# The inverse transform of a depthwise convolution written with tokens on partitions, its LayerNorm there, and transposes back

## The chip, the cores and the metric

The kernel runs on one core of a Trainium2 chip. The metric is the device time of one execution in microseconds (us), as the median of the runs. Engines are named as in the profile: PE is TensorE (PEld its weight loads), DVE VectorE, ACT ScalarE, POOL GpSimd, SP the engine whose queue issues most of the DMAs.

## What is computed

Two layers over 512 tokens of width 1024 (8 grid rows of 64 tokens). Layer 0 is a gated recurrence, and the change leaves it alone. Layer 1 is a convolution module; from the reference, cut:

```python
def _conv_mixer(h, w_in, b_in, dw, dw_b, ln_g, ln_b, w_out, b_out, conv_fn):
    p = h @ w_in + b_in
    a, gl, gate = jnp.split(p, 3, axis=-1)          # 2048 channels each
    u = a * jax.nn.sigmoid(gl)
    u = conv_fn(u, dw, dw_b)                        # 31 taps along each grid row of 64 tokens, plus dw_b
    u = jax.nn.silu(_layernorm(u, ln_g, ln_b))      # mean and variance over the 2048 channels
    return (u * jax.nn.silu(gate)) @ w_out + b_out
...
    x = x + gate[:, None] * y
...
return _rmsnorm(x, final_norm_g)
```

## The kernel before

All data is float32. A product that must be exact to float32 is made of three products of two parts each (`hi`, `lo`, type float32r); a few small products are plain float32 matmuls, which the profile shows as two passes, so two rows for one matmul.

Layer 1 (from line 656) works in four groups `g` of 512 channels:

- **Two halves of the input projection** (lines 679 to 701): `part` 1 is the gate `gl`, `part` 0 the value `a`. Each has 96 products of 128x512 into four PSUM banks `pa{part}_{g}_{t}`, one for each 128 tokens `t`. The pool `pa` has four banks, so the first product of the next half needs the first bank to have been read. Weights come in four pieces `ci{part}_{g}_{kq}`: a DMA on SP into `raw`, a copy to `hi` on ACT (line 139), a subtraction to `lo` on POOL or DVE (line 141). `raw`, `hi` and `lo` have three buffers each.
- **The reading of the banks** (lines 702 to 716, DVE and ACT) adds the biases of the group, which lie in the tile `bb`: `bb[:, 1]` for `gl` (line 704, into `sgl`), `bb[:, 0]` for `a` (line 710, into `ta`). `bb` has one buffer; a DMA that POOL issues (line 675) fills it with the group's 512 channels, the same for all partitions. Then `u` is made, one tile for each grid row, with the high part of the row on one half of the partitions and the low part on the other.
- **The transform** (lines 718 to 723): for each grid row `r` a bank `pf` gets two products, one with `f_hi` over all 128 partitions, one with `f_lo` over the 64 partitions of the high part. DVE multiplies it with the transformed taps `wt`, which gives `pr` (118 x 512).
- **The inverse** (lines 724 to 734): for each 128 channels `ct` a bank `pi` gets eight products, 128 columns of `pr` as weights and the 64 columns of `inv` moving. The channels are then on partitions. ACT adds the bias, DVE sums `s1` for the mean.

Two pieces of a modulation vector (`ada_piece`, lines 170 to 180: a DMA into `raw`, a chain of eight DVE instructions `adacc`, a product `adbps`) follow in each group.

After the groups comes the **LayerNorm** (lines 741 to 763): the mean is a product with `ones` over `s1`, then 16 subtractions (DVE), 16 squares (ACT), 14 additions on DVE and POOL, two products `var`, a logarithm and an exponential, 16 multiplications (DVE) and 16 SiLUs (ACT). The **gate path** (lines 767 to 781) has 24 products `pgt` for each of 16 tiles `ct`; its weights `cg` are split with `lo` on POOL. `z = gate * y` goes, in two parts, into the output projection `cop` (line 824 on).

A scheduler sets the order of instructions on each engine. It puts the transform and inverse of group `g` between the input products of group `g + 1`, and those of group 3 between the first gate products.

## Time and profile before

| | |
|---|---|
| median of 3 runs | 1392.67 us (1392.63 to 1394.99) |
| span of the profiled execution | 1389.6 us |
| PE busy | 1332.2 us, 96% of the span |
| DVE, ACT, POOL busy | 962.8, 637.4, 368.9 us |
| mean granted clock of PE | 0.986 of full |
| DMA | 119 MB, mean 86 GB/s |

The page gives the span of the profiled execution, from its first to its last instruction, and no time of its own beside it; the median of the three runs is 3.07 us above that span. A busy PE is one with at least one matmul in its pipeline: the distance from one matmul's start to the next one's start tells what a matmul costs, the duration in a row is longer.

### The profile page before, as it was taken

Reading aid. Unit: us, or ns where it says so; the run is one execution under the profiler, and the core shown is the slowest. Engines: PE = TensorE matmul, PEld = TensorE weight load, DVE = VectorE, ACT = ScalarE, POOL = GpSimd, SP = SyncE. Lnnn points to the kernel's source line nnn. Section 1 sums busy time; section 2 is a strip of 40 time slices with the busy share of each in tenths; the row PEclk is TensorE's granted clock in tenths of the full one; section 3 lists DMA queues with packets and bytes.
Section 4 is the critical chain, followed back from the end, with each engine's and each line's share of the span. In section 5 each row is a group of like instructions: output and inputs, shape, how many; then the busy total and the mean of one; then the engine's idle time right before and its main releaser. Section 6 shows DMA issues by size and latency. Waiting matters only on the chain.

```text
span 1389.6 us, 18990 instructions
## 1 busy us (share of the span) xinstructions
PE 1332.2 (96%) x7530; PEld 1124.9 (81%) x7530; DVE 962.8 (69%) x1486; ACT 637.4 (46%) x965; POOL 368.9 (27%) x302
## 2 busy tenths in 40 slices
PE   6999999999999999999999999999999999986997
PEld 2588988998888898888898889867787877865887
DVE  8868787896687786787688777756656747278323
ACT  6455553562355354465345455443223333458321
POOL 3222241240240151140033133122211213267221
PEclk9999999999999999999999999999999999998999
DMA  9312113114112312212211312023422322120321
...
DMA packets 35720, 119.05 MB, mean 86 GB/s; under 512 B 4562, under 2 KB 6898, under 8 KB 35632
## 3 DMA queue, kind: packets, MB, share of 16 engines
...
## 4 chain that ended last, share of the span: by engine, by line
PE 61%; DVE 22%; ACT 5%; DMA 4%; POOL 4%; issue 3%; SPq 0%; DVEq 0%; ACTq 0%; POOLq 0%
PE pa L688 4%; PE pa L689 4%; PE pa L693 4%; PE pz L301 2%; PE pz L302 2%; PE pz L304 2%; PE pi L728 2%; PE cop L842 2%; PE cop L846 2%; PE cop L843 2%; PE op L530 2%; PE h_sc L465 2%; DVE adacc L176 2%; PE op L532 2%; PE op L531 2%
## 5 line engine op out<-in xcount | busy, mean ns | idle before, releaser
L688 PE MATMUL pa<-ci_hi,h_hi 128*128 128x512 f32 x256 | 99.6, 398 | 1.9 <-ACT h_hi L649 1.9
L689 PE MATMUL pa<-ci_lo,h_hi 128*128 128x512 f32 x256 | 100.4, 396 | 0.0
L116 POOL TENSOR_SCALAR sg<-sg 128x1536 f32<-128x1536 f32 x16 | 76.6, 4787 | 70.7 <-ACT sg L549 70.5
L301 PE MATMUL pz<-h_hi,wz_hi 128*128 128x512 f32 x232 | 93.3, 402 | 0.8 <-ACT wz_hi L139 0.8
L302 PE MATMUL pz<-h_lo,wz_hi 128*128 128x512 f32 x232 | 92.9, 401 | 0.0
L176 DVE SCALAR_TENSOR_TENSOR adacc<-adb,sc,adacc 128x128 f32<-128x128 f32 x224 | 82.0, 384 | 3.6
L141 POOL TENSOR_TENSOR ci_lo<-ci_raw,ci_hi 128x1024 fp32r<-128x1024 f32 x18 | 44.5, 2472 | 144.4 <-ACT ci_hi L139 124.6
L141 POOL TENSOR_TENSOR cg_lo<-cg_raw,cg_hi 128x1024 fp32r<-128x1024 f32 x16 | 62.2, 3889 | 66.9 <-PE pgt L774 28.2
L139 ACT ACTIVATE ci_hi<-ci_raw 128x1024 fp32r<-128x1024 f32 x29 | 30.7, 1059 | 93.8 <-PE pa L693 53.6
L693 PE MATMUL pa<-ci_hi,h_lo 128*128 128x512 f32 x224 | 72.1, 400 | 0.0
L312 PE MATMUL pv<-wv_hi,h_hi 128*128 128x256 f32 x256 | 64.8, 288 | 0.0
L313 PE MATMUL pv<-wv_hi,h_lo 128*128 128x256 f32 x256 | 64.1, 286 | 0.0
L400 POOL TENSOR_TENSOR h_f<-h_fac 128x16 f32<-128x16 f32 x16 | 10.0, 627 | 198.6 <-DVE h_kl L446 147.1
L304 PE MATMUL pz<-h_hi,wz_lo 128*128 128x512 f32 x232 | 61.3, 399 | 0.0
L432 DVE SCALAR_TENSOR_TENSOR h_S<-h_S,h_dec,h_kb 128x128 f32<-128x128 f32 x96 | 48.7, 507 | 18.0 <-ACT h_kb L426 16.9
L139 ACT ACTIVATE wz_hi<-wz_raw 128x1024 fp32r<-128x1024 f32 x29 | 30.7, 1057 | 64.6 <-DMA wz_raw<-in_w_in 51.7
L302 PE MATMUL pc<-hc,wz_hi 128*128 128x256 f32 x232 | 60.1, 291 | 0.0
L301 PE MATMUL pc<-hc,wz_hi 128*128 128x256 f32 x232 | 59.7, 289 | 0.0
L688 PEld LDWEIGHTS pa<-ci_hi,h_hi 128*128 128x128 f32 x256 | 48.2, 188 | 13.5 <-issue 2.7
L141 DVE TENSOR_TENSOR wz_lo<-wz_raw,wz_hi 128x1024 fp32r<-128x1024 f32 x29 | 35.4, 1222 | 32.3 <-ACT wz_hi L139 32.1
L689 PEld LDWEIGHTS pa<-ci_lo,h_hi 128*128 128x128 f32 x256 | 48.2, 188 | 11.3 <-issue 0.7
L377 POOL TENSOR_TENSOR h_ref<-h_tot,h_gt 128x64 f32<-128x64 f32 x16 | 17.5, 1091 | 146.4 <-DVE h_ref L404 136.7
...
## 6 DMA issues: line engine op xcount, KB each, us to landing
adb<-in_ada_c SPq DMA_DIRECT2D x32, 512.0 KB, 3.4
ci_raw<-in_c_in SPq DMA_DIRECT2D x32, 512.0 KB, 3.4
wz_raw<-in_w_in SPq DMA_DIRECT2D x29, 512.0 KB, 3.4
ada<-in_ada_a SPq DMA_DIRECT2D x16, 512.0 KB, 7.2
wv_raw<-in_w_v SPq DMA_DIRECT2D x16, 512.0 KB, 3.4
wg_raw<-in_w_in SPq DMA_DIRECT2D x16, 512.0 KB, 3.4
cg_raw<-in_c_gate SPq DMA_DIRECT2D x16, 512.0 KB, 3.5
co_raw<-in_c_out SPq DMA_DIRECT2D x16, 512.0 KB, 3.5
```

The costliest lines, as they stand in the source:

```text
L116: (G if pool_min else V).tensor_scalar(out=t, in0=t, scalar1=EMAX, scalar2=None, op0=ALU.min)
L139: act(out=hi, in_=raw, func=AF.Copy)
L141: lo_eng.tensor_tensor(out=lo, in0=raw, in1=hi.bitcast(F32), op=ALU.subtract)
L176: V.scalar_tensor_tensor(out=acc, in0=raw[:, k, :], scalar=sc[:, k, 0:1], in1=acc, op0=ALU.mult, op1=ALU.add)
L301: mm(ps[:, :T], lhsT=hi[:, k, :], rhs=rhi[k], start=(k == 0), stop=False)
L302: mm(ps[:, :T], lhsT=hi[:, k, :], rhs=rlo[k], start=False, stop=False)
L304: mm(ps[:, :T], lhsT=lo[:, k, :], rhs=rhi[k], start=False, stop=(k == KD - 1))
L312: mm(ps[:, :256], lhsT=lhi[k][:, c], rhs=hi[:, k % 4, :], start=(k == 0), stop=False)
L313: mm(ps[:, :256], lhsT=llo[k][:, c], rhs=hi[:, k % 4, :], start=False, stop=False)
L688: mm(pss[t], lhsT=h_hi[:, 2 * kq + k, c], rhs=hi[:, k, :], start=(kq == 0 and k == 0), stop=False)
L689: mm(pss[t], lhsT=h_hi[:, 2 * kq + k, c], rhs=lo[:, k, :], start=False, stop=False)
L693: mm(pss[t], lhsT=h_lo[:, 2 * kq + k, c], rhs=hi[:, k, :], start=False, stop=(kq == 3 and k == 1))
```

## The change

Of layer 1 alone, and of the host's layout of one small array:

- `f_lo` becomes a tile of two matrices with zeros in the half that isn't wanted, so that both products of the transform run over all 128 partitions.
- The inverse has `inv` as weights and `pr` as moving operand. Two grid rows go to the two column halves of the array and so to the two partition halves of one bank `py`; tokens are then on partitions. Two matmuls of 64x512 for a bank of 128 tokens stand for eight of 128x64 for a bank of 128 channels.
- The bias of the convolution is added by DVE from a third row of `bb`, `bb[:, 2]`; `bb` grows from 512 to 768 KB and still has one buffer.
- Mean and variance come from `bn_stats` and `bn_aggr`; 16 `tensor_scalar` normalise. The products `mean` and `var`, the squares and the sums are gone.
- Each `ct` has four TensorE transposes into a bank `pt`, which ACT reads with the SiLU.
- Every second `lo` of the gate weights moves from POOL to DVE; `gate` has 4 buffers where it had 8 and 8; the pool of `y` has 20 where it had 16.

```diff
-        f_lo = p1.tile([P, P], F32R, name="f_lo")
+        f_lo = p1.tile([P, 2, P], F32R, name="f_lo")
+        V.memset(f_lo.bitcast(F32), 0.0)
         V.tensor_copy(out=f_hi, in_=fraw)
-        V.tensor_tensor(out=f_lo, in0=fraw, in1=f_hi.bitcast(F32), op=ALU.subtract)
+        for i in range(2):
+            o = slice(i * GRID, (i + 1) * GRID)
+            V.tensor_tensor(out=f_lo[o, i, :], in0=fraw[o], in1=f_hi[o].bitcast(F32), op=ALU.subtract)
+        eye1 = p1.tile([P, P], F32, name="eye1")
+        nc.sync.dma_start(out=eye1, in_=consts[:, C_IDN:C_IDN + P])
...
-                bb = pu.tile([P, 2, 512], F32, name=f"bb{g}", tag="bb", bufs=1)
+                bb = pu.tile([P, 3, 512], F32, name=f"bb{g}", tag="bb", bufs=1)
                 nc.gpsimd.dma_start(out=bb, in_=c_bab[:, :, g * 512:(g + 1) * 512].partition_broadcast(P))
...
-                for r in range(ROWS):
-                    ps = pf.tile([P, 512], F32, name=f"pf{g}_{r}", tag="pf")
-                    o = slice((r % 2) * GRID, (r % 2 + 1) * GRID)
-                    mm(ps, lhsT=f_hi, rhs=u[r], start=True, stop=False)
-                    mm(ps, lhsT=f_lo[o, :], rhs=u[r][o, :], start=False, stop=True)
-                    V.tensor_tensor(out=pr[r][:NR], in0=ps[:NR], in1=wt[g][:NR], op=ALU.mult)
-                for i in range(4):
-                    ct = 4 * g + i
-                    ps = pm.tile([P, 512], F32, name=f"pi{ct}", tag="ms")
-                    for r in range(ROWS):
-                        mm(ps[:, r * GRID:(r + 1) * GRID], lhsT=pr[r][:NR, i * P:(i + 1) * P], rhs=inv[:NR, :], start=True, stop=True)
-                    y.append(p1.tile([P, L], F32, name=f"y{ct}", tag="y", bufs=NH))
-                    act(out=y[ct], in_=ps, func=AF.Identity, bias=ccols[:, 0, ct:ct + 1])
-                    ...
+                for t in range(NB):
+                    py = pm.tile([P, 512], F32, name=f"py{g}_{t}", tag="ms")
+                    for i in range(2):
+                        r = 2 * t + i
+                        ps = pf.tile([P, 512], F32, name=f"pf{g}_{r}", tag="pf")
+                        mm(ps, lhsT=f_hi, rhs=u[r], start=True, stop=False)
+                        mm(ps, lhsT=f_lo[:, i, :], rhs=u[r], start=False, stop=True)
+                        pr = pu.tile([P, 512], F32, name=f"pr{g}_{r}", tag="pr", bufs=8)
+                        V.tensor_tensor(out=pr[:NR], in0=ps[:NR], in1=wt[g][:NR], op=ALU.mult)
+                        mm(py[i * GRID:(i + 1) * GRID], lhsT=inv[:NR, :], rhs=pr[:NR], start=True, stop=True)
+                    yt[t, g] = p1.tile([P, 512], F32, name=f"yt{g}_{t}", tag="y", bufs=20)
+                    V.tensor_tensor(out=yt[t, g], in0=py, in1=bb[:, 2, :], op=ALU.add)
+                    V.bn_stats(out=stats[t][:, g, :], in_=yt[t, g])
...
-        (mean, 16 subtractions, 16 squares, 14 additions, var, 16 multiplications, 16 SiLUs)
+        for t in range(NB):
+            V.bn_aggr(out=mv[:, t, :], in_=stats[t].rearrange("p a b -> p (a b)"))
+        act(out=rst, in_=mv[:, :, 1:2], func=AF.Ln, bias=eps)
+        act(out=rst, in_=rst, func=AF.Exp, scale=-0.5)
+        for g in range(4):
+            for t in range(NB):
+                V.tensor_scalar(out=yt[t, g], in0=yt[t, g], scalar1=mv[:, t, 0:1], scalar2=rst[:, t, :], op0=ALU.subtract, op1=ALU.mult)
...
-            w = wpiece(c_gate[ct], [KD, P], f"cg{ct}", G)
+            w = wpiece(c_gate[ct], [KD, P], f"cg{ct}", (V, G)[ct % 2])
...
+            ps = pm.tile([P, 512], F32, name=f"pt{ct}", tag="ms")
+            for t in range(NB):
+                nc.tensor.transpose(ps[:, t * P:(t + 1) * P], yt[t, ct // 4][:, (ct % 4) * P:(ct % 4 + 1) * P], eye1)
+            y = pg.tile([P, L], F32, name=f"y{ct}", tag="yc", bufs=4)
+            act(out=y, in_=ps, func=AF.Silu, scale=ccols[:, 2, ct:ct + 1], bias=ccols[:, 3, ct:ct + 1])
```

How the scheduler's order moves, at three places. Line numbers after the change are 6 higher up to the biases' additions (704 and 710 become 710 and 716), and L733 is the product `py`, L735 the addition into `yt`.

PE, where `part` 1 of group 1 (banks `pa_1_0` to `pa_1_3`) ends and `part` 0 begins with its first bank; before:

```order
L689 MATMUL pa_1_3_9014<-ci_1_3_lo,h_hi 128x512
L693 MATMUL pa_1_3_9014<-ci_1_3_hi,h_lo 128x512 x2
L688 MATMUL pa_1_0_9143<-ci_1_0_hi,h_hi 128x512
L689 MATMUL pa_1_0_9143<-ci_1_0_lo,h_hi 128x512
L728 MATMUL pi_8921<-tr,pr_6_8887 128x64
L728 MATMUL pi_8933<-tr,pr_6_8887 128x64
```

and after the change:

```order
L699 MATMUL pa_1_3_8997<-ci_1_3_hi,h_lo 128x512 x2
L733 MATMUL py_3_8936<-pr_6_8940,tr 64x512
L178 MATMUL adbps_8963<-ones,adacc_8954 128x1
L733 MATMUL py_3_8936<-pr_7_8946,tr 64x512
L178 MATMUL adbps_8977<-ones,adacc_8968 128x1
L694 MATMUL pa_1_0_9126<-ci_1_0_hi,h_hi 128x512
L695 MATMUL pa_1_0_9126<-ci_1_0_lo,h_hi 128x512
```

The last inverse product of group 0 now stands between the two parts, and `part` 0 starts right behind it. Groups 1 and 2 read alike.

The queues of POOL and DVE at the same place (names with all numbers; the first digit of `ci` is the part, the last the piece). POOL before:

```order
L141 TENSOR_TENSOR ci1_1_2_lo_9079<-ci1_1_2_raw_9075,ci1_1_2_hi_9077 128x1024
L675 DMA bb1_8997<-in_c_bab 128x2x512
L141 TENSOR_TENSOR ci0_1_0_lo_9151<-ci0_1_0_raw_9147,ci0_1_0_hi_9149 128x1024
L141 TENSOR_TENSOR ci0_1_2_lo_9211<-ci0_1_2_raw_9207,ci0_1_2_hi_9209 128x1024
L141 TENSOR_TENSOR ci1_2_0_lo_9433<-ci1_2_0_raw_9429,ci1_2_0_hi_9431 128x1024
```

POOL after:

```order
L141 TENSOR_TENSOR ci1_1_2_lo_9062<-ci1_1_2_raw_9058,ci1_1_2_hi_9060 128x1024
L141 TENSOR_TENSOR ci0_1_0_lo_9134<-ci0_1_0_raw_9130,ci0_1_0_hi_9132 128x1024
L141 TENSOR_TENSOR ci0_1_2_lo_9194<-ci0_1_2_raw_9190,ci0_1_2_hi_9192 128x1024
L681 DMA bb1_8980<-in_c_bab 128x3x512
L141 TENSOR_TENSOR ci1_2_0_lo_9392<-ci1_2_0_raw_9388,ci1_2_0_hi_9390 128x1024
```

The load of `bb` for group 1 has moved behind the weight pieces of `part` 0. DVE after, from the last addition that reads `bb0` to the first that reads `bb1` (`adacc27` is the chain of a modulation piece whose DMA also lands here):

```order
L735 TENSOR_TENSOR yt0_3_8949<-py0_3_8936,bb0_8590 128x512
L176 SCALAR_TENSOR_TENSOR adacc26_9344<-adb26_9342,sc_100,adacc26_9344 128x128
L180 TENSOR_TENSOR adac_113<-adbps25_8977,ab_88 128x1
L736 BN_STATS st3_8586<-yt0_3_8949 128x6
L176 SCALAR_TENSOR_TENSOR adacc26_9344<-adb26_9342,sc_100,adacc26_9344 128x128 x6
L174 TENSOR_SCALAR adacc27_9358<-adb27_9356,sc_100 128x128
L176 SCALAR_TENSOR_TENSOR adacc27_9358<-adb27_9356,sc_100,adacc27_9358 128x128 x5
L710 TENSOR_TENSOR sgl1_0_8982<-pa1_1_0_8994,bb1_8980 128x512
L710 TENSOR_TENSOR sgl1_1_8983<-pa1_1_1_8995,bb1_8980 128x512
```

Before, the last reader of `bb0` was the addition of line 710 for the fourth 128 tokens of group 0, some 14 instructions ahead of the first reader of `bb1` on DVE.

PE among the input products of group 1, after the change, where an inverse product stands alone:

```order
L695 MATMUL pa_1_3_8997<-ci_1_1_lo,h_hi 128x512
L733 MATMUL py_0_8888<-pr_0_8892,tr 64x512
L729 MATMUL pf_2_8905<-u_2_8598,f_hi 128x512
L730 MATMUL pf_2_8905<-u_2_8598,f_lo 128x512
L694 MATMUL pa_1_3_8997<-ci_1_1_hi,h_hi 128x512
L695 MATMUL pa_1_3_8997<-ci_1_1_lo,h_hi 128x512
L733 MATMUL py_0_8888<-pr_1_8898,tr 64x512
L729 MATMUL pf_3_8911<-u_3_8599,f_hi 128x512
```

Its two halves are four products of the whole array apart. In group 3 the last `py` stands among the first products of the gate tile `ct` 4, and 31 gate products follow it before the first transpose; in the order before, 271 of the 384 gate products stood behind the last inverse product.

## Rows read from the trace of the kernel before

**Rows 1.** The page: busy time of the engines, and the chain that ended last by engine.

```profile
PE 1332.2 (96%) x7530; PEld 1124.9 (81%) x7530; DVE 962.8 (69%) x1486; ACT 637.4 (46%) x965; POOL 368.9 (27%) x302
...
PE 61%; DVE 22%; ACT 5%; DMA 4%; POOL 4%; issue 3%; SPq 0%; DVEq 0%; ACTq 0%; POOLq 0%
```

**Rows 2.** The chain of waits from 1202 to 1291 us, from the end of the last inverse product to the first product of the output projection: start, time on the chain, engine, tile, line, count.

```profile
1202.46 1.68 PE pgt L774 x7
...
1209.45 0.86 PE mean L742 x2
...
1242.63 2.08 PE var L756 x2
1244.70 2.12 PE pgt L774 x7
...
1262.55 1.87 PE pgt L774 x8
1264.45 21.72 POOL cg_lo L141
1286.22 3.78 PE pgt L774 x8
1290.00 0.55 PE cop L842 x2
```

**Rows 3.** PE in order of time: the last column says how long PE sat idle before, and for whom.

```profile
1242.63 2.08 PE L756 MATMUL var<-s,ones 128*128 128x512 f32 x2 [5.25 <-DVE s L754]
...
1286.22 3.78 PE L774 MATMUL pgt<-h_hi,cg_lo 128*128 128x512 f32 x8 [12.51 <-POOL cg_lo L141]
```

**Rows 4.** PE in stretches of 2 us: length, busy time, granted clock (1.00 is full), DMA share, GB/s.

```profile
1274.00:1276.00 2.00, 0.00 (x0) 1.00 0.00 0
...
1278.00:1280.00 2.00, 0.00 (x0) 0.50 0.00 0
...
1288.00:1290.00 2.00, 2.00 (x6) 0.50 0.61 207
1290.00:1292.00 2.00, 2.00 (x10) 0.99 0.98 363
```

**Rows 5.** PE in order of time around two transform pairs of group 3 (start, duration; 64*128 says that the weights fill 64 rows and 128 columns).

```profile
1180.39 0.66 PE L728 MATMUL pi<-tr,pr 118*128 118x64 f32 x4
1180.86 0.48 PE L721 MATMUL pf<-u,f_hi 128*128 128x512 f32 x1
1181.27 0.50 PE L722 MATMUL pf<-u,f_lo 64*128 64x512 f32 x1
1181.70 0.66 PE L728 MATMUL pi<-tr,pr 118*128 118x64 f32 x4
```

**Rows 6.** The chain of waits, two pieces of PE: ten plain float32 passes of 512 columns, and 32 passes of the inverse (start, time on the chain, count).

```profile
932.02 4.29 PE r_ss L629 x10
...
1023.88 3.52 PE pi L728 x32
```

**Rows 7.** PE in order of time at the start of layer 0: products with two or four weight columns (128*2) among products of the whole array.

```profile
46.28 1.32 PE L251 MATMUL pe<-h_hi,we_hi 128*128 128x512 f32 x5
47.44 0.63 PE L156 MATMUL adaps<-ada_lo,sc 128*2 128x512 f32 x2
47.91 0.39 PE L252 MATMUL pe<-h_lo,we_hi 128*128 128x512 f32 x1
48.14 0.39 PE L253 MATMUL pe<-h_hi,we_lo 128*128 128x512 f32 x1
```

**Rows 8.** PE in order of time around four transposes of 128x128 in layer 0 (line 354).

```profile
121.97 2.02 PE L304 MATMUL pg<-h_hi,wg_lo 128*128 128x512 f32 x8
123.83 0.60 PE L354 MATMUL h_ct<-kc,h_ec 128*128 128x128 f32 x4
124.26 1.95 PE L465 MATMUL h_sc<-h_ql,h_kl 128*128 128x128 f32 x16
```

**Rows 9.** The tile `bb`: DVE's last reading of group 0's, POOL's issue of group 1's load, DVE's first reading of group 1's (in order of time), and the loads' time from issue to landing over all four.

```profile
990.70 0.68 DVE L710 TENSOR_TENSOR ta<-pa,bb 128x512 f32<-128x512 f32 x1
...
991.67 0.73 POOL L675 DMA_DIRECT2D bb<-in_c_bab  x1 [1.44 <-DVE ta L710]
...
1011.10 0.68 DVE L704 TENSOR_TENSOR sgl<-pa,bb 128x512 f32<-128x512 f32 x1
...
DMA to landing us min/median/max: 5.1/5.4/6.0
```

**Rows 10.** Groups of instructions from 940 to 1200 us, ACT and POOL: the two steps that split a weight piece (count, busy us, mean ns, idle before).

```profile
L139 ACT ACTIVATE ci_hi<-ci_raw 128x1024 fp32r<-128x1024 f32 x29 | 30.7, 1059 | 93.8 <-PE pa L693 53.6 <-issue 28.0 <-PE pa L699 9.1
...
L141 POOL TENSOR_TENSOR ci_lo<-ci_raw,ci_hi 128x1024 fp32r<-128x1024 f32 x15 | 37.0, 2464 | 144.4 <-ACT ci_hi L139 124.6 <-DMA ci_raw<-in_c_in 19.8
```

**Rows 11.** DVE: additions from PSUM, the two kinds of the modulation chain (min/median/max ns) and its load, and a `tensor_scalar` of 128x512.

```profile
L710 DVE TENSOR_TENSOR ta<-pa,bb 128x512 f32<-128x512 f32 x16 | 10.7, 685 | 1.1 <-PE pa L693 0.9
...
L176 DVE SCALAR_TENSOR_TENSOR adacc<-adb,sc,adacc x56: 337/352/2489, 967.6 to 1156.9; 128x128 f32<-128x128 f32 x56
...
L174 DVE TENSOR_SCALAR adacc<-adb,sc x8: 275/278/336, 967.2 to 1151.8; 128x128 f32<-128x128 f32 x8
...
adb<-in_ada_c SPq DMA_DIRECT2D x32, 512.0 KB, 3.4
...
L202 DVE TENSOR_SCALAR xn<-xn,mod_g,mod_s 128x512 f32<-128x512 f32 x8 | 4.2, 541 | 1.1 <-ACT h_hi L201 1.1
```

**Rows 12.** ACT in order of time between the logarithm and the exponential of the LayerNorm.

```profile
1252.51 1.28 ACT L760 ACT_TABLE_LOAD   x1
1253.80 0.63 ACT L760 ACTIVATE rstd<-rstd 128x512 f32<-128x512 f32 x1
```

More of the change, by code (lines that the diff above doesn't have):

```diff
@@ L665, in hybrid_kernel @@
         f_hi = p1.tile([P, P], F32R, name="f_hi")
-        f_lo = p1.tile([P, P], F32R, name="f_lo")
+        f_lo = p1.tile([P, 2, P], F32R, name="f_lo")
+        V.memset(f_lo.bitcast(F32), 0.0)
         V.tensor_copy(out=f_hi, in_=fraw)
-        V.tensor_tensor(out=f_lo, in0=fraw, in1=f_hi.bitcast(F32), op=ALU.subtract)
-        y = []
-        s1 = p1.tile([P, L], F32, name="s1")
+        for i in range(2):
[3 more added lines that the diff above has]
+        nc.sync.dma_start(out=eye1, in_=consts[:, C_IDN:C_IDN + P])
+        yt = {}
+        stats = [p1.tile([P, 4, 6], F32, name=f"st{t}") for t in range(NB)]
         with tc.tile_pool(name="pu", bufs=1) as pu:
             for g in range(4):
-                bb = pu.tile([P, 2, 512], F32, name=f"bb{g}", tag="bb", bufs=1)
+                bb = pu.tile([P, 3, 512], F32, name=f"bb{g}", tag="bb", bufs=1)
                 nc.gpsimd.dma_start(out=bb, in_=c_bab[:, :, g * 512:(g + 1) * 512].partition_broadcast(P))
@@ L716, in hybrid_kernel @@
                                 V.tensor_tensor(out=u[r][other], in0=ta[own], in1=u[r][own].bitcast(F32), op=ALU.subtract)
-                pr = [pu.tile([P, 512], F32, name=f"pr{g}_{r}", tag="pr", bufs=8) for r in range(ROWS)]
-                for r in range(ROWS):
-                    ps = pf.tile([P, 512], F32, name=f"pf{g}_{r}", tag="pf")
-                    o = slice((r % 2) * GRID, (r % 2 + 1) * GRID)
-                    mm(ps, lhsT=f_hi, rhs=u[r], start=True, stop=False)
-                    mm(ps, lhsT=f_lo[o, :], rhs=u[r][o, :], start=False, stop=True)
-                    V.tensor_tensor(out=pr[r][:NR], in0=ps[:NR], in1=wt[g][:NR], op=ALU.mult)
@@ L739, in hybrid_kernel @@
         pg = l1.enter_context(tc.tile_pool(name="pg", bufs=1))
-        ps = pm.tile([P, 512], F32, name="mean", tag="ms")
-        mm(ps, lhsT=ones, rhs=s1, start=True, stop=True)
-        mean = pg.tile([P, L], F32, name="mean_sb")
-        act(out=mean, in_=ps, func=AF.Copy, scale=1.0 / E2)
-        s2 = [pg.tile([P, L], F32, name=f"s2_{i}") for i in range(2)]
-        for ct in range(NH):
-            V.tensor_tensor(out=y[ct], in0=y[ct], in1=mean, op=ALU.subtract)
-            acc, eng = s2[ct % 2], (V, G)[ct % 2]
-            if ct < 2:
-                act(out=acc, in_=y[ct], func=AF.Square)
-            else:
-                sq = pg.tile([P, L], F32, name=f"sq{ct}", tag="lsq", bufs=4)
-                act(out=sq, in_=y[ct], func=AF.Square)
-                eng.tensor_tensor(out=acc, in0=acc, in1=sq, op=ALU.add)
-        ps = pm.tile([P, 512], F32, name="var", tag="ms")
-        mm(ps, lhsT=ones, rhs=s2[0], start=True, stop=False)
-        mm(ps, lhsT=ones, rhs=s2[1], start=False, stop=True)
-        rstd = pg.tile([P, L], F32, name="rstd")
-        act(out=rstd, in_=ps, func=AF.Ln, scale=1.0 / E2, bias=eps)
-        act(out=rstd, in_=rstd, func=AF.Exp, scale=-0.5)
-        for ct in range(NH):
-            V.tensor_tensor(out=y[ct], in0=y[ct], in1=rstd, op=ALU.mult)
-            act(out=y[ct], in_=y[ct], func=AF.Silu, scale=ccols[:, 2, ct:ct + 1], bias=ccols[:, 3, ct:ct + 1])
+        mv = pg.tile([P, NB, 2], F32, name="mv")
+        for t in range(NB):
+            V.bn_aggr(out=mv[:, t, :], in_=stats[t].rearrange("p a b -> p (a b)"))
+        rst = pg.tile([P, NB, 1], F32, name="rst")
+        act(out=rst, in_=mv[:, :, 1:2], func=AF.Ln, bias=eps)
[3 more added lines that the diff above has]
+                V.tensor_scalar(out=yt[t, g], in0=yt[t, g], scalar1=mv[:, t, 0:1], scalar2=rst[:, t, :], op0=ALU.subtract, op1=ALU.mult)
+        rstd = pg.tile([P, L], F32, name="rstd")
         zhi, zlo = [], []
@@ L774, in hybrid_kernel @@
                 mm(ps, lhsT=w[1][:, k, :], rhs=h_hi[:, k, :], start=False, stop=(k == KD - 1))
-            gate = (p1 if ct < 8 else pg).tile([P, L], F32, name=f"gate{ct}", tag="gate", bufs=8)
+            gate = p1.tile([P, L], F32, name=f"gate{ct}", tag="gate", bufs=4)
             act(out=gate, in_=ps, func=AF.Silu, bias=ccols[:, 1, ct:ct + 1])
-            V.tensor_tensor(out=gate, in0=gate, in1=y[ct], op=ALU.mult)
-            zhi.append(p1.tile([P, L], F32R, name=f"zhi{ct}", tag="y", bufs=NH))
+            ps = pm.tile([P, 512], F32, name=f"pt{ct}", tag="ms")
[3 more added lines that the diff above has]
+            act(out=y, in_=ps, func=AF.Silu, scale=ccols[:, 2, ct:ct + 1], bias=ccols[:, 3, ct:ct + 1])
+            V.tensor_tensor(out=gate, in0=gate, in1=y, op=ALU.mult)
+            zhi.append(p1.tile([P, L], F32R, name=f"zhi{ct}", tag="y", bufs=20))
             act(out=zhi[ct], in_=gate, func=AF.Copy)
@@ L909, in _layout @@
     d["c_in"] = ci[:, :, :, 0:2].transpose(3, 4, 0, 2, 1, 5)
-    d["c_bab"] = conv_b_in[0, :2 * E2].reshape(1, 2, E2)
+    d["c_bab"] = np.concatenate([conv_b_in[0, :2 * E2], conv_dw_b[0]]).reshape(1, 3, E2)
     d["c_gate"] = conv_w_in[0][:, 2 * E2:].reshape(KD, P, NH, P).transpose(2, 1, 0, 3)
```

4 lines of the change are left out of this document (removed).

## The prediction

> **What bounds the kernel now.** I read the page first: PE is busy 96% of the span and has 61% of the chain that ended last [rows 1]. So an edit is worth what it takes from PE's queue or from PE's idle time, and work on DVE, ACT or POOL costs something only where PE comes to wait for it. Next I read the chain of waits through the LayerNorm [rows 2]: PE does gate products there all the time, and the chain leaves PE only once, for 21.72 us of `cg_lo` on POOL. PE in order of time gives the two idle stretches: 5.25 us ahead of `var`, which waits for DVE's sums, and 12.51 us ahead of a gate product, which waits for that `cg_lo` [rows 3]. Then I read the clock: it is full at the start of the second idle stretch, 0.50 while PE stands still, and stays there until 1290.00, 3.8 us after PE has begun again [rows 4]. Idle time of PE costs more here than its own length: eight gate products took 3.78 us at half clock and 1.87 at full [rows 2], so a restart gives away 1.9 us.
>
> **The change, part by part.** The sum is made against the profiled execution, whose span is 1389.6 us; the median, 1392.67, stands 3.07 above it. I add what I find to the median, since the few us around the span do not change.
>
> *Transform.* A gate product costs 1.87/8 = 0.233 us [rows 2], and two would be 0.467. The pair with `f_hi` and the half-height `f_lo` goes from 1180.86 to 1181.70, 0.84 us [rows 5]: 0.37 more than its columns cost. The half-height product brings that, and with zeros in the other half both are full-height. 32 pairs x 0.37 = **-11.9**. The smallest gain is none, if the 0.37 came with the switch to plain float32 behind the pair; the rows put the gap between `f_hi` and the next kind, so I take it whole.
>
> *Inverse.* Removed: 16 tiles of 16 passes; 32 passes cost 3.52 us [rows 6], so 256 cost 28.2. Added: 4 groups x 4 banks x 2 halves x 2 passes = 64 passes of 512 columns; ten such passes took 4.29 us [rows 6], so 64 cost 27.5. **-0.7**. The trace has no plain product on half the columns of the array. The nearest rows from one side are products with two to four weight columns among products of the full array: 47.44 to 47.91 for two, 47.91 to 48.14 for the next, 0.23 each, nothing for the change of shape [rows 7]. From the other side it is the half-height product, 0.37 a visit [rows 5], 32 x 0.37 = 11.9. I take nothing: rows 7 are the ones in which columns are cut, as here. In sentences of its own: the Trainium skill, "TensorEngine Tiling (Array Packing)", section "Key Properties", says that a change of tiling mode drains TensorE. By it every lone `py` half would drain, and the term would be +11.9 by the price of the half-height product; rows 5 agree with it, rows 7 do not.
>
> *LayerNorm.* From 1202.46 to 1290.00 are 87.54 us [rows 2]. The idle time is 5.25 + 12.51 = 17.8 [rows 3]. To it I add what ran above its normal price: 1.9 in the eight products behind the idle time, 1.2 in `var` (2.08, where two passes cost 0.86, as `mean` does) and 0.5 in the seven products behind it (2.12 against 1.63). Together **-21.4**, if nothing in the new order waits. The products `mean` and `var`, six passes x 0.429: **-2.6**. The idle time goes because the 21.72 us of POOL go: every second `lo` is DVE's, and DVE has lost 16 subtractions and the sums. What is late next is the chain from the last `py` to the first transpose: addition 0.69 [rows 11], statistics 0.5 to 0.7 (estimated between `tensor_scalar` and an addition from PSUM [rows 11]), aggregation some 0.3 (like the smallest DVE steps of rows 11), a logarithm and exponential with a table load of 1.28 between [rows 12] and some 0.3 each, one normalisation 0.54 [rows 11] and the hops: 5 us. It is covered by the 31 gate products that the order puts there, 31 x 0.233 = 7.2 us. If the cover fails, by three more normalisations or other DVE work ahead, it costs 0 to 6; I take **+1.0**.
>
> *Transposes.* Added: 64 of 128x128; four took 123.83 to 124.26 [rows 8], 0.108 each: **+6.9**. ACT's 16 SiLUs only change their source. 16 `tensor_scalar` of 0.54 on DVE, 8.7 us, stand beside the 24-product gate tiles of 5.6 us each; only the first four of each group are wanted at once.
>
> *Zeros, identity, constants.* One memset, one more subtraction, one DMA, all at the beginning: nothing, beside the loads there.
>
> So far: -11.9 - 0.7 - 21.4 - 2.6 + 6.9 + 1.0 = **-28.7**.
>
> *The tile `bb`.* This is the edit that looks like nothing. `bb` has one buffer. In the trace DVE reads group 0's for the last time at 990.70, POOL issues the load at 991.67, it lands 5 to 6 us later, and is wanted at 1011.10: 14 us to spare [rows 9]. Now the last reader is the addition into `yt` for the last 128 tokens, behind the last `py`; the order of PE puts that `py` exactly between `part` 1 and `part` 0 of the next group. The first product of `part` 0 needs the first bank of `part` 1 to be read by the addition of line 710, and that addition needs the new `bb`. So at each of three boundaries PE stands still from the end of `py` until a load that can only be issued behind it has landed.
>
> I count from Tp, the start of the last `py`. PE has two halves of 0.86 [rows 6] and two small products: busy until Tp + 2.0. The load stands on POOL's queue behind the `lo` of the third piece of `part` 0. `hi` has three buffers, so that piece takes the one which the last products of `part` 1 have just let go: the ACT copy 1.06, the POOL subtraction 2.46 [rows 10], with hops Tp + 3.9. Then the load. 512 KB took 5.1 to 6.0 [rows 9]; 768 KB I estimate at 6.4, between 5.1 (only latency) and 8.1 (5.4 x 1.5): Tp + 10.3. On DVE the addition also stands behind the chain `adacc27`, whose own load takes 3.4, and six steps of 0.28 to 0.35 [rows 11], which would end between Tp + 9 and Tp + 12; I let it end with the load. The addition, 0.69 [rows 11], and a hop: PE begins again at Tp + 11.5. Idle 9.5 us, and 1.9 for a restart at half clock [rows 2, 4]: 11.4 x 3 = **+34.2**. Bounds: 7.0 idle (load 5.1, POOL's step ahead of it earlier by one us, restart 0) x 3 = 21.0, or 26.1 with a restart of 1.7; 10.9 + 1.9 = 12.8 x 3 = 38.4.
>
> **Sum:** -28.7 + 34.2 = +5.5; 1392.67 + 5.5 = **1398** us. The gain and the wait are each some thirty us, and what is forecast is their difference; it changes sign where a boundary costs 28.7/3 = 9.6 us.
>
> **The rivals.**
>
> *A short reload (faster).* If the load is issued right behind the addition into `yt` (POOL done by then), lands in 5.1 us and the clock is back at once, a boundary costs 7 to 9 us: -28.7 + 3 x 8 = -4.7, so 1388 (1385 to 1390). It decides from 9.6 us per boundary downward. For it: loads of 512 KB have landed in 5.1 us [rows 9]. Against it: POOL's subtraction waits for the same buffer that PE lets go at that very moment, POOL takes 2.46 for it [rows 10], and a restart has cost 1.9. Chance 0.20.
>
> *Column halves drain the array.* If each of the 32 `py` halves costs 0.37 like the half-height product [rows 5], +11.9 comes on top: 1398 + 12 = 1410. For it: rows 5; the halves stand alone among full products, four apart. Against it: rows 7. This is what the rule of the Trainium skill, "TensorEngine Tiling (Array Packing)", "Key Properties", would do. Chance 0.18.
>
> *The LayerNorm's chain is late.* If the chain behind the last `py` takes 13 instead of 5 us (POOL and DVE both busy with weight pieces and modulation chains), PE waits 6 in place of 1: about 1404. The 7.2 us of cover speak against it. Chance 0.06.
>
> *The halves work at the same time.* The change uses two column halves as if both could run together; if they did, the 27.5 us would halve: 1398 - 13.7 = 1384. Against it: in the order they stand four full products apart, and no two rows of this trace overlap so. Chance 0.06.
>
> **How the numbers follow.** My forecast, a boundary wait of 10 to 13 us and no drain, has 0.50, with a range of its own from 1393 to 1404: 1392.67 - 28.7 + 3 x 9.7 = 1393, and 1392.67 - 28.7 + 38.4 = 1402, with 2 for the 0 to 6 of the LayerNorm chain. The range given goes from 1386 (inside the short reload, near its lower end) to 1411 (the drain on top of the forecast). It leaves out the overlap of halves, the last us of the short reload, and a drain together with the largest wait. The three chances go by 0.2%, 2.8 us, about what a measurement of this kernel can tell from no change: below 1389.9 are most of the short reload and the overlap, together 0.16; from 1389.9 to 1395.5 the rest of the short reload and the lower end of my forecast, 0.20; above, 0.64.
>
> **What would show it.** Right: in PE's order of time three idle stretches of 9 to 10 us, each behind the last `py` of groups 0, 1 and 2 and ended by DVE's `sgl`, with the load of `bb` landing just ahead; the clock at 0.50 in and behind them; pairs of `pf` 0.47 us from start to start of the next; `py` halves of 0.86 with 0.23 behind them; transposes of 0.11; no idle time of more than a few us between the last `py` and the output projection. Wrong: if `bb` lands before PE reaches the boundary, or the idle stretches are under 7 us, the sum is too high by up to 34; if PE waits at the first `pt`, or for a `cg_lo` again, the -21.4 fails; if the product behind a `py` half starts 0.3 to 0.4 us late each time, the drain is there.

## The result, and the profile after

The change takes **1410.95 us** (median of 4 runs, 1408.67 to 1411.43) where the kernel before takes 1392.65: 1.013 times as long, with an interval of 1.0113 to 1.0147. The profiled execution took 1408.67 us, with a span of 1406.6 (before: 1392.67 and 1389.6), so the two profiles below stand 17.0 us apart in span. The time lies 0.05 us inside the upper end of the range, on the number that the prediction gave to its second rival (1410), and not on its forecast (1398). Four executions of kernels of this study took 1469 to 4207 us where the others of the same kernel agree; the times below are medians without them.

The page after, busy time by engine, to be read against [rows 1]:

```profile
PE 1335.0 (95%) x7396; PEld 1107.9 (79%) x7396; DVE 953.6 (68%) x1493; ACT 617.7 (44%) x932; POOL 318.6 (23%) x287
```

PE is busy 3 us longer with fewer instructions, and idle for 14 more. To see where, read first and last starts on PE by tile: minimum, median and maximum duration in ns, then the first and the last start. Before:

```profile
L688 PE MATMUL pa<-ci_hi,h_hi x256: 390/394/483, 940.1 to 1161.2; 128*128 128x512 f32 x128
L771 PE MATMUL pgt<-h_hi,cg_hi x128: 390/392/480, 1162.1 to 1273.1; 128*128 128x512 f32 x128
L842 PE MATMUL cop<-zhi,co_hi x160: 277/389/513, 1289.8 to 1378.8; 128*128 128x512 f32 x96, 128*128 128x256 f32 x64
```

and after:

```profile
L694 PE MATMUL pa<-ci_hi,h_hi x256: 387/393/767, 935.5 to 1194.3; 128*128 128x512 f32 x128
L760 PE MATMUL pgt<-h_hi,cg_hi x128: 390/396/505, 1195.2 to 1303.0; 128*128 128x512 f32 x128
L836 PE MATMUL cop<-zhi,co_hi x160: 276/393/476, 1305.7 to 1395.9; 128*128 128x512 f32 x96, 128*128 128x256 f32 x64
```

| stretch | before | after | difference |
|---|---|---|---|
| layer 0, to the first `pa` (not changed) | 940.1 | 935.5 | -4.6 |
| input products, first `pa` to first `pgt` | 222.0 | 259.7 | +37.7 |
| gate stage with the LayerNorm, first `pgt` to first `cop` | 127.7 | 110.5 | -17.2 |
| output projection to the end | 99.8 | 100.9 | +1.1 |

The layer 0 difference is not the change's: in the ten other traces that this document reads, the one before among them, the same stretch is 935.1 to 940.6. So the change gains 17 us in the gate stage and loses 38 in the input products. What PE waits for, in total, times, longest, after:

```profile
PE pa L694 <- DVE sgl L710: 32.9, 3, 11.3
```

Both waits of [rows 3] are gone, and one of 32.9 us in three parts has come. The first of the three boundaries, PE in order of time:

```profile
1015.22 1.07 PE L733 MATMUL py<-pr,tr 118*64 118x512 f32 x2
1016.23 0.38 PE L178 MATMUL adbps<-ones,adacc 128*128 128x1 f32 x2
1016.54 1.07 PE L733 MATMUL py<-pr,tr 118*64 118x512 f32 x2
1017.54 0.38 PE L178 MATMUL adbps<-ones,adacc 128*128 128x1 f32 x2
1028.66 0.76 PE L694 MATMUL pa<-ci_hi,h_hi 128*128 128x512 f32 x1 [10.74 <-DVE sgl L710]
...
1032.08 0.39 PE L694 MATMUL pa<-ci_hi,h_hi 128*128 128x512 f32 x1
...
1099.81 0.77 PE L694 MATMUL pa<-ci_hi,h_hi 128*128 128x512 f32 x1 [11.27 <-DVE sgl L710]
...
1170.81 0.77 PE L694 MATMUL pa<-ci_hi,h_hi 128*128 128x512 f32 x1 [10.88 <-DVE sgl L710]
```

The last two rows are the same place at the second and the third boundary.

DVE at the first boundary:

```profile
1016.72 2.17 DVE L174 TENSOR_SCALAR adacc<-adb,sc 128x128 f32<-128x128 f32 x1
1018.81 0.68 DVE L735 TENSOR_TENSOR yt<-py,bb 128x512 f32<-128x512 f32 x1
...
1027.83 2.48 DVE L710 TENSOR_TENSOR sgl<-pa,bb 128x512 f32<-128x512 f32 x4 [3.09 <-DMA bb<-in_c_bab]
```

POOL:

```profile
1016.46 2.34 POOL L141 TENSOR_TENSOR ci_lo<-ci_raw,ci_hi 128x1024 fp32r<-128x1024 f32 x1 [14.90 <-ACT ci_hi L139]
1019.78 0.79 POOL L681 DMA_DIRECT2D bb<-in_c_bab  x1 [0.98 <-DVE adacc L176]
```

And the loads of `bb`: count, size, median us from issue to landing (the four took 7.3 to 8.6):

```profile
bb<-in_c_bab POOLq DMA_DIRECT2D x4, 768.0 KB, 8.1
```

This is the wait that the prediction described, step by step: the last reader of the old `bb` (1018.81), the load (1019.78, landed 1027.8), the addition of `sgl`, PE. The granted clock (third number from the end, ahead of DMA share and GB/s) falls to the lower of its two levels, 1.2 of 2.4 GHz, while PE stands still, and comes back here 3.4 us after PE has begun:

```profile
1022.00:1024.00 2.00, 0.00 (x0) 0.00 (x0) 1.82 (x7) 0.00 (x0) 0.00 (x0) 0.50 0.80 217
...
1032.00:1034.00 2.00, 2.00 (x10) 1.61 (x10) 0.00 (x0) 0.00 (x0) 0.00 (x0) 1.00 0.67 248
```

Eight products from 1028.66 to 1032.08 took 3.42 us, 1.55 more than eight at full clock. This is the shortest of the three restarts: the 24 products behind each wait took 7.12, 7.38 and 7.69 us where 24 at full clock take 5.6 (24 x 1.87/8), so the restarts lose 1.5, 1.8 and 2.1 us, 5.4 together. The three boundaries cost 32.9 + 5.4 = 38.3 us, 12.8 each.

The second loss is smaller and spread. A lone half of `py`, PE in order of time:

```profile
993.30 0.40 PE L695 MATMUL pa<-ci_lo,h_hi 128*128 128x512 f32 x1
993.63 1.07 PE L733 MATMUL py<-pr,tr 118*64 118x512 f32 x2
994.63 0.50 PE L729 MATMUL pf<-u,f_hi 128*128 128x512 f32 x1
994.97 0.39 PE L730 MATMUL pf<-u,f_lo 128*128 128x512 f32 x1
```

From 993.30 to 994.97 are 1.67 us; two products and two passes are 2 x 0.233 + 0.858 = 1.32. The half starts 0.10 late, is 0.14 longer, and the product behind it holds its successor back by 0.11: 0.35 us for one half. The 26 halves that stand away from the three boundaries read 0.34 to 0.44 each; the two at each boundary stand right ahead of the wait, and own_tile below, where PE does not wait there, shows the same price for them. 32 x 0.35 = 11.2 us in all.

In the gate stage, the last of the first four transposes and eight later ones, PE in order of time:

```profile
1241.32 0.33 PE L768 MATMUL pt<-eye,yt 128*128 128x128 f32 x1 [0.18 <-DVE yt L751]
...
1247.52 1.03 PE L768 MATMUL pt<-eye,yt 128*128 128x128 f32 x8
1248.31 1.63 PE L763 MATMUL pgt<-h_hi,cg_lo 128*128 128x512 f32 x6
```

and the `lo` of the gate weights on POOL (minimum, median and maximum ns, first and last start), before and after:

```profile
L141 POOL TENSOR_TENSOR cg_lo<-cg_raw,cg_hi x16: 2357/2406/25122, 1152.1 to 1261.0; 128x1024 fp32r<-128x1024 f32 x16
...
L141 POOL TENSOR_TENSOR cg_lo<-cg_raw,cg_hi x8: 2375/2402/2808, 1191.0 to 1287.5; 128x1024 fp32r<-128x1024 f32 x8
```

PE waits 0.18 us for the LayerNorm's chain and for nothing else. Eight transposes take 0.79 us start to start, and no `cg_lo` on POOL is longer than 2.8 us, where one had 25 before.

### The profile page after: what moved, and what is told of

It is laid out like the page before. It is cut to its first block, busy times and chain, and to the rows that moved or that the text cites. A ratio compares the mean times of both kernels' runs of the same rounds, so it can differ in the third digit from the quotient of the medians.

```text
span 1406.6 us, 18673 instructions
## 1 busy us (share of the span) xinstructions
PE 1335.0 (95%) x7396; PEld 1107.9 (79%) x7396; DVE 953.6 (68%) x1493; ACT 617.7 (44%) x932; POOL 318.6 (23%) x287
## 4 chain that ended last, share of the span: by engine, by line
PE 63%; DVE 22%; DMA 5%; ACT 5%; issue 3%; POOL 2%; SPq 0%; DVEq 0%; ACTq 0%
PE pa L694 5%; PE pa L695 4%; PE pa L699 4%; PE pz L301 3%; PE pz L302 2%; PE pz L304 2%; PE op L530 2%; PE cop L836 2%; PE cop L840 2%; PE pgt L763 2%; PE cop L837 2%; PE op L532 2%; PE op L531 2%; PE py L733 2%; PE pgt L760 2%
## 5 line engine op out<-in xcount | busy, mean ns | idle before, releaser
L694 PE MATMUL pa<-ci_hi,h_hi 128*128 128x512 f32 x256 | 102.4, 409 | 34.8 <-DVE sgl L710 32.9
L695 PE MATMUL pa<-ci_lo,h_hi 128*128 128x512 f32 x256 | 103.3, 407 | 0.0
L176 DVE SCALAR_TENSOR_TENSOR adacc<-adb,sc,adacc 128x128 f32<-128x128 f32 x224 | 76.1, 355 | 3.7
L836 PE MATMUL cop<-zhi,co_hi 128*128 128x512 f32 (+1 forms) x160 | 54.2, 352 | 0.0
L760 PE MATMUL pgt<-h_hi,cg_hi 128*128 128x512 f32 x128 | 51.4, 402 | 0.0
```

The lines of the kernel that those rows point to most:

```text
L176: V.scalar_tensor_tensor(out=acc, in0=raw[:, k, :], scalar=sc[:, k, 0:1], in1=acc, op0=ALU.mult, op1=ALU.add)
L694: mm(pss[t], lhsT=h_hi[:, 2 * kq + k, c], rhs=hi[:, k, :], start=(kq == 0 and k == 0), stop=False)
L695: mm(pss[t], lhsT=h_hi[:, 2 * kq + k, c], rhs=lo[:, k, :], start=False, stop=False)
L760: mm(ps, lhsT=w[0][:, k, :], rhs=h_hi[:, k, :], start=(k == 0), stop=False)
L836: mm(ps, lhsT=hi[:, i, c], rhs=zhi[ct][:, tok], start=(ct == 0), stop=False)
```

## The experiments

**own_tile.** Undoes the shared buffer alone:

```diff
-                bb = pu.tile([P, 3, 512], F32, name=f"bb{g}", tag="bb", bufs=1)
-                nc.gpsimd.dma_start(out=bb, in_=c_bab[:, :, g * 512:(g + 1) * 512].partition_broadcast(P))
+                bb = pu.tile([P, 2, 512], F32, name=f"bb{g}", tag="bb", bufs=1)
+                nc.gpsimd.dma_start(out=bb, in_=c_bab[:, 0:2, g * 512:(g + 1) * 512].partition_broadcast(P))
+                bc = pu.tile([P, 1, 512], F32, name=f"bc{g}", tag="bc", bufs=2)
+                nc.gpsimd.dma_start(out=bc, in_=c_bab[:, 2:3, g * 512:(g + 1) * 512].partition_broadcast(P))
...
-                    V.tensor_tensor(out=yt[t, g], in0=py, in1=bb[:, 2, :], op=ALU.add)
+                    V.tensor_tensor(out=yt[t, g], in0=py, in1=bc[:, 0, :], op=ALU.add)
```

> The convolution bias gets a tile of its own (two buffers, loaded from POOL's queue) and bb goes back to two rows. My theory: the three idle stretches behind the last py of groups 0 to 2 (10.7, 10.9 and 11.3 us, 32.9 in all) and the half-clock stretch behind each (eight products in 3.4 us where 1.9 is the price at full clock, so 1.6 each) come only from the reload of bb, so all of 32.9 + 4.7 = 37.6 us goes: 1411 - 37.6 = 1373 (1369 to 1378), no idle time before the first product of part 0. Rival: another wait stands right behind that one (the weight piece whose split ends 3.6 us behind the last py starts, or the modulation chain on DVE): 3 to 6 us per boundary stay and the clock falls as before, 1384 to 1397.

Measured: 1371.66 us (1371.47 to 1373.53), 0.9855 of before (0.9839 to 0.9871), 39.3 below the change, where the theory had 37.6 and the rows above give 38.3. From the start of layer 1 PE waits for nothing over 2 us; `sgl` is not in the list of its waits, and behind the last `py` of group 0 the next product starts 1.00 us after it (1022.80 to 1023.80). The wait for `bb`, with the half clock behind it, is all of the boundary's cost, and no other wait stood behind it.

**bias_by_sp.** Who issues the load:

```diff
-                nc.gpsimd.dma_start(out=bb, in_=c_bab[:, :, g * 512:(g + 1) * 512].partition_broadcast(P))
+                nc.sync.dma_start(out=bb, in_=c_bab[:, :, g * 512:(g + 1) * 512].partition_broadcast(P))
```

> The load of bb (three rows, one buffer, as in the change) is issued from SP's queue instead of POOL's; the scheduler also puts the modulation chain behind the readers of bb at the boundary. First theory: 8.1 us is what the load takes from POOL's queue beside a busy DVE, and from SP's queue it takes about 1.5 x 3.5 = 5.3 us (512 KB land in 3.5 from there): 2.8 us less at each of three boundaries, 8 in all, 1403 (1400 to 1406). Rival: the 8.1 us are the price of 768 KB to all partitions whoever issues (5.4 x 1.5 = 8.1): landing 7.5 to 8.5, 1411 (1408 to 1413).

Measured: 1411.08 us (1409.24 to 1412.13). The load's time to landing (the last number), in this kernel:

```profile
bb<-in_c_bab SPq DMA_DIRECT2D x4, 768.0 KB, 8.1
```

and in own_tile:

```profile
bb<-in_c_bab POOLq DMA_DIRECT2D x4, 512.0 KB, 5.6
```

The first theory falls: 8.1 us is what this load to all partitions takes at 768 KB in this place, from either queue, and PE's three waits are 32.4 us. The price does not go with the size throughout: the 256 KB of `bc` in own_tile landed in 5.2 us, nearly as late as 512 KB. So 5.4 x 1.5 gave the right number here, but it is not shown to be a rule.

**first_step_on_act.** Line 174 took 2.17 us at each boundary, 0.28 elsewhere [rows 11]:

```diff
-        V.tensor_scalar(out=acc, in0=raw[:, 0, :], scalar1=sc[:, 0, 0:1], scalar2=None, op0=ALU.mult)
+        act(out=acc, in_=raw[:, 0, :], func=AF.Copy, scale=sc[:, 0, 0:1])
```

(in layer 1 only)

> The change with the first step of each modulation piece of this layer on ACT instead of DVE. In the change's trace that step (line 174) took 2.17 us at each of the three boundaries, where 0.28 is usual, and ended when POOL's split of a weight piece ended; the addition that releases bb stands behind it on DVE. Theory: the step waits for POOL; without it the addition runs right behind the last py, the load of bb is issued 3.7 us behind that py's start instead of 4.5, and each boundary is 0.8 us shorter: 1411 - 2.5 = 1408.5 (1407 to 1410). Rival: whatever DVE does first there is held up (the addition takes the 2.2 us itself): issue at 4.5 as before, 1411.

Measured: 1407.58 us (1404.1 to 1410.61). DVE and then POOL at the first boundary, whose last `py` starts at 1014.68:

```profile
1017.11 0.69 DVE L738 TENSOR_TENSOR yt<-py,bb 128x512 f32<-128x512 f32 x1 [0.84 <-PE py L736]
```

```profile
1015.92 2.35 POOL L141 TENSOR_TENSOR ci_lo<-ci_raw,ci_hi 128x1024 fp32r<-128x1024 f32 x1 [14.89 <-ACT ci_hi L139]
1018.21 0.79 POOL L684 DMA_DIRECT2D bb<-in_c_bab  x1
```

The load is issued 3.5 us behind the start of the last `py`, not 4.6 (1015.22 to 1019.78 in the change), and PE's three waits are 29.8 us instead of 32.9. The step on DVE waited for POOL's subtraction; without it, the load waits for that subtraction on POOL's own queue, as the prediction had it. The runs differ by more than this gain, so the rows carry the verdict, not the median.

**full_array.** The same inverse without column halves:

```diff
...
-                        mm(py[i * GRID:(i + 1) * GRID], lhsT=inv[:NR, :], rhs=pr[:NR], start=True, stop=True)
+                        mm(py, lhsT=inv2[:NR, i, :], rhs=pr[:NR], start=(i == 0), stop=(i == 1))
```

(`inv2`: two matrices of 118x128, `inv` in one half of the columns, zeros in the other)

> The inverse's weights are padded with zeros to 128 columns, one matrix for each half, and the two products accumulate in the bank: the same columns streamed, but the whole array instead of a half. First theory: the 0.35 us that each py half costs above its two passes (1.67 us from the product ahead of it to the second product of the next pair, where 0.233 + 0.858 + 0.233 = 1.32 is the price) is the change to a 64-column tile and back: 32 x 0.35 = 11 us go, 1411 - 11 = 1400 (1398 to 1402), and the product behind a py follows after 0.86 + 0.0. Rival: the 0.35 us belongs to the change from the float32r products to the two-pass float32 ones, which stays: 1411 (1409 to 1413).

Measured: 1405.87 us (1402.8 to 1407.45), 5 below the change, between the two theories and inside the range of neither. PE in order of time tells why:

```profile
998.18 0.40 PE L699 MATMUL pa<-ci_lo,h_hi 128*128 128x512 f32 x1
998.42 1.02 PE L737 MATMUL py<-pr,inv 118*128 118x512 f32 x2
998.88 0.80 PE L733 MATMUL pf<-u,f_hi 128*128 128x512 f32 x1
999.51 0.40 PE L734 MATMUL pf<-u,f_lo 128*128 128x512 f32 x1
```

The same stretch is 1.33 us, as much as its columns: the 0.35 us belongs to the half-width tile, not to plain float32 among float32r. But the wait for `bb` grew from 32.9 to 35.9, about 1.0 us at each boundary. PE begins to wait some 0.5 us earlier there, because the `py` in front is shorter, and the load is issued 5.2 us behind the start of the last `py`, not 4.6: the order on DVE has one more step of a modulation chain ahead of the addition that releases `bb`, and that step (line 176) takes 2.3 us, until POOL's subtraction ends, where 0.35 is usual. In the gate stage, where no such wait follows, 110.5 became 107.9: 2.6 for 8 halves.

**halves_together.** The two halves right behind one another:

```diff
...
-                        mm(py[i * GRID:(i + 1) * GRID], lhsT=inv[:NR, :], rhs=pr[:NR], start=True, stop=True)
...
+                    one = mm(py[GRID:P], lhsT=inv[:NR, :], rhs=prs[1][:NR], start=True, stop=True)
+                    with tc.issue_after(one.ins):
+                        mm(py[0:GRID], lhsT=inv[:NR, :], rhs=prs[0][:NR], start=True, stop=True)
```

> The two halves of a py stand right behind one another on PE (second row's half first), nothing else is changed. If a change of tile shape costs 0.35 us per visit, there are 16 visits instead of 32: -5.6 us, but the last py of a group then waits about 1 us for its taps' product, three times: 1405 to 1409, and a pair of halves takes 2 x 0.86 = 1.7 us. If the two halves can run beside each other in the array, a pair takes about 0.9 us: another 16 x 0.86 = 13.7 less, 1392 to 1396. If each half drains whatever stands beside it: 1411 to 1414.

Measured: 1391.08 us (1386.53 to 1394.64; 0.9992 of before, 0.9974 to 1.001), 20 below the change. This is the theory of two halves beside each other, a us under its range, and the other two fall. The same kernel once more, in one execution, for the rows:

> The kernel of halves_together again, for a profile at the chip's usual pace. If the halves run beside each other: both passes of a pair start within 0.05 us of each other, 1.2 us for a pair with what stands around it, the idle time at the three boundaries is 10 to 13 us each as in the change, and the time is 1388 to 1394.

Measured: 1391.77 us. The last pair of group 0 and the boundary behind it:

```profile
1015.10 0.64 PE L735 MATMUL py<-pr,tr 118*64 118x512 f32 x1 [0.79 <-DVE pr L733]
1015.10 0.64 PE L737 MATMUL py<-pr,tr 118*64 118x512 f32 x1
...
1026.52 0.77 PE L694 MATMUL pa<-ci_hi,h_hi 128*128 128x512 f32 x1 [9.17 <-DVE sgl L710]
```

Both halves start their first pass in the same hundredth of a microsecond: two column halves run at the same time when nothing stands between them. The wait at a boundary was 9.2, 9.1 and 9.0 us, less than I expected (10 to 13). The pair in front waits 0.79 for its own operand, so POOL's subtraction is over when the pair ends; line 174 takes its 0.28, and the load is issued 2.1 us behind the start of the pair.

**own_together.** Both edits, own_tile and halves_together.

> Both at once: the convolution bias in a tile of its own (as in own_tile, 1371.7 us) and the two halves of a py right behind one another (as in halves_together, 19 us below the change). Theory: adjacent halves run beside each other in the array, so a pair costs 0.86 + 0.35 = 1.21 us where two lone halves cost 2.42: 16 x 1.21 = 19.3 us less, and it has nothing to do with the wait for bb: 1371.7 - 19.3 = 1352 (1349 to 1356); in PE's order of time the two halves start within 0.05 us of each other. Rival: part of the 19 us was idle time at the boundaries that the other order shortened: 1358 to 1366.

Measured: 1352.53 us (1350.51 to 1352.73), **0.9722 of before** (0.9709 to 0.9735): the fastest of the study. One pair:

```profile
1002.63 0.40 PE L701 MATMUL pa<-ci_hi,h_lo 128*128 128x512 f32 x1
1002.96 0.64 PE L737 MATMUL py<-pr,tr 118*64 118x512 f32 x1
1002.96 0.64 PE L739 MATMUL py<-pr,tr 118*64 118x512 f32 x1
...
1003.97 0.50 PE L732 MATMUL pf<-u,f_hi 128*128 128x512 f32 x1
1004.30 0.39 PE L733 MATMUL pf<-u,f_lo 128*128 128x512 f32 x1
```

From 1002.63 to 1004.30 are 1.67 us, exactly what one lone half took with its two neighbours. The gain of 19.1 us against own_tile (19.3 expected) is 16 halves that now cost nothing. No wait for `bb` was left in own_tile, so the rival, which put part of the gain down to idle time at the boundaries, falls too.

**f_lo_full_height.** One edit of the change on the kernel before:

```diff
...
-                    mm(ps, lhsT=f_lo[o, :], rhs=u[r][o, :], start=False, stop=True)
+                    mm(ps, lhsT=f_lo[:, r % 2, :], rhs=u[r], start=False, stop=True)
```

> The kernel before with one edit of the change: f_lo as two matrices with zeros, so that both products of the transform have 128 rows. Theory: the half-height product costs 0.37 us a pair above its columns: 1392 - 11.9 = 1380 (1378 to 1383), pairs of pf 0.47 us long. Rival: the 0.37 comes with the change to the plain float32 products of the inverse that follow most pairs, and stays: 1390 to 1393.

Measured: 1377.64 us, 0.9907 of before (0.9893 to 0.992): -13.5 where -11.9 was forecast. A pair among the passes of the inverse:

```profile
1171.94 0.48 PE L724 MATMUL pf<-u,f_hi 128*128 128x512 f32 x1
1172.26 0.39 PE L725 MATMUL pf<-u,f_lo 128*128 128x512 f32 x1
1172.49 0.55 PE L731 MATMUL pi<-tr,pr 118*128 118x64 f32 x4
1172.86 0.48 PE L774 MATMUL pgt<-h_hi,cg_hi 128*128 128x512 f32 x1
```

A pair takes 0.55 from its start to the next kind's, where [rows 5] had 0.84, and the four passes behind it 0.37, where they had 0.47. The gap is the half-height tile's.

**split_lo_gate.** The other edit on the kernel before:

```diff
-            w = wpiece(c_gate[ct], [KD, P], f"cg{ct}", G)
+            w = wpiece(c_gate[ct], [KD, P], f"cg{ct}", (V, G)[ct % 2])
```

> The kernel before with one edit of the change: every second lo of the gate weights on DVE. Theory: the 21.7 us of POOL on the chain go, and with them 12.5 us of idle time and 1.9 us of half clock: 1392 - 14.4 = 1378 (1375 to 1381), the wait for var (5.3 us) stays. Rival: DVE has the sixteen subtractions and the sums of the LayerNorm at the same place, and eight more steps of 1.2 us make var and what follows later by as much: 1384 to 1392.

Measured: 1387.66 us, 0.9977 of before (0.9966 to 0.9989): only -3.5. PE, at the end of the wait that should have gone:

```profile
1284.54 3.78 PE L774 MATMUL pgt<-h_hi,cg_lo 128*128 128x512 f32 x8 [9.53 <-POOL cg_lo L141]
```

The `lo` steps left on POOL:

```profile
L141 POOL TENSOR_TENSOR cg_lo<-cg_raw,cg_hi x8: 2383/2406/19938, 1160.4 to 1264.5; 128x1024 fp32r<-128x1024 f32 x8
```

and a stretch of 10 us ahead of that wait: busy time (and instructions) of PE, PEld, DVE, ACT and POOL, granted clock, DMA share, GB/s:

```profile
1270.00:1280.00 10.00, 5.01 (x22) 3.74 (x20) 10.00 (x17) 8.90 (x16) 10.00 (x1) 1.00 0.00 0
```

One `cg_lo` on POOL still lasts 19.9 us (1264.54 to 1284.48): in that stretch DVE is busy 10.00 of 10.00 us with 17 steps, POOL with one. DVE's steps there:

```profile
1265.41 6.10 DVE L777 TENSOR_TENSOR gate<-gate,y 128x512 f32<-128x512 f32 x10
1271.44 3.09 DVE L781 TENSOR_TENSOR zl<-gate,zhi 128x512 fp32r<-128x512 f32 x5
```

My theory, which is also the prediction's first reason, fell. The time lies in the rival's range (1384 to 1392), but its detail, a later `var`, did not come: that wait is 4.2 us.

**gate_lo_on_pool.** The other way round, in the change:

```diff
-            w = wpiece(c_gate[ct], [KD, P], f"cg{ct}", (V, G)[ct % 2])
+            w = wpiece(c_gate[ct], [KD, P], f"cg{ct}", G)
```

> The change with all sixteen lo of the gate weights on POOL, as in the kernel before. Theory after split_lo_gate: what made one cg_lo 18 to 25 us long was DVE's row of LayerNorm steps without a pause, not the number of lo on POOL; the change has few of those, so no cg_lo takes more than 5 us, PE does not wait for one by over a us, and the time stays: 1411 (1409 to 1413). Rival (what the prediction gave as the reason): without the split POOL falls behind again, one cg_lo of 15 to 25 us and 10 to 14 us of idle time and half clock come back: 1421 to 1426.

Measured: 1413.26 us (1409.85 to 1415.82), 1.0141 of before (1.01 to 1.0183), which can't be told from the change's 1.013; in its profile 1.3 us more in the gate stage than the change (111.8 for 110.5). The `lo` steps on POOL:

```profile
L141 POOL TENSOR_TENSOR cg_lo<-cg_raw,cg_hi x16: 2392/2401/5805, 1190.0 to 1292.2; 128x1024 fp32r<-128x1024 f32 x16
```

With all sixteen on POOL the longest takes 5.8 us, a little over the 5 that I expected, and no wait for one comes back. The two runs make four cases: with the old LayerNorm one `cg_lo` takes 25 us without the split and 20 with it, with the new one 5.8 and 2.8. So what lengthened it was DVE's row of steps without a pause, which goes with the old LayerNorm. The rows of split_lo_gate name the steps: they are not the LayerNorm's own, but the products `gate * y` and the subtractions for `zl` and `zlo`, which pile up behind it because all 16 `y` become free in one go. In the change `y` comes tile by tile from the transposes, and the same steps stand a few at a time, with pauses: DVE is busy 4 to 8 of 10 us there (1250 to 1290). That this spacing is the cause is read from the rows; no run changed it alone. The split is worth about a microsecond of the 17.8 us of idle time that went.

## Why the prediction was right or wrong, step by step

The time lies in the range, and the way it moved was forecast, but that the number is inside is luck. What happened is a drain together with the largest wait, which the prediction says its range leaves out: with the measured prices below its sum gives -28.7 + 38.3 + 11.2 - 0.8 = +20.0, so 1392.7 + 20.0 = 1412.7, above the 1411 where the range ends. The measured median is 1.7 below that.

**The boundary (+34.2): right, the largest term.** The place, the chain and its coming three times came out as written. It cost 38.3, almost the upper bound (38.4), and own_tile took 39 back. Two sizes were off. The load takes 8.1 us, not 6.4: the upper bound, from 5.4 x 1.5, was the price, and bias_by_sp shows that it does not hang on the queue. And it is issued at Tp + 4.6 rather than 3.9, because line 174 holds up the addition. A third error went the other way: PE is busy until Tp + 2.7 and not 2.0, since the halves drain, and so has 0.7 us less to wait. The restart, 1.5 to 2.1, was priced well at 1.9.

**The column halves (0): wrong, and the step that failed.** "I take nothing: rows 7 are the ones in which columns are cut, as here." The products of [rows 7] have two weight columns (128*2; the two-or-four in its heading is more than its rows show) and pay nothing for it; `py` has 64 (118*64) and pays. Fewer columns alone are thus not what costs, and no run here tried a width between 4 and 64. The row that had to be taken was the half-height product [rows 5]: 0.37 there, 0.35 measured here, 11.2 us in all (11.9 in the rival). The rival with a chance of 0.18 happened, together with the forecast's boundary. The rule of the Trainium skill, "TensorEngine Tiling (Array Packing)", section "Key Properties", that a change of tiling mode drains TensorE, held: full_array without the tile has no such gap.

**The halves at the same time: right for this change, wrong as a judgement of what could be had.** They did not overlap, being four products apart. Placed together they do, for 19 us. The same section says that different tiles can load weights and multiply in parallel, and own_together agrees, with starts in the same 0.01 us.

**The LayerNorm stage (-21.4, -2.6): the sum right, the reason wrong.** With the transposes (+6.9), a quarter of the transform's gain (-3.0), of the inverse (-0.2), the chain's +1.0 and, now, of the drains (+2.8) the gate stage should change by -16.5; it changed by -17.2. The idle time went, but for neither of the two reasons given. The split of the `lo` steps is worth about 1 us of it (split_lo_gate, gate_lo_on_pool), and the 16 subtractions and the sums that DVE lost stood ahead of `var`, before the long `cg_lo` began. It went because DVE's steps behind the LayerNorm no longer come in one row. The chain behind the last `py` cost PE 0.18 us, not 1.0.

**Transform (-11.9): right**; -13.5 by itself in f_lo_full_height. **Transposes: right**, 0.79 us for eight.

Put together by the profiles, the +20.0 stands against the 21.6 by which everything from the first `pa` on grew. What is left is about 1.5 in the first half of group 0, where the products start at half clock after an idle time of 1.88 us (before, after 1.87, they did not), 1.1 in the output projection, whose products came every 0.233 us instead of 0.227, and -1.6 if the transform's gain was the 13.5 of its own run. Why the clock and the output projection differ, no run here settles.
